# Moving the second gate's modulation vector from the first stage of an encoder layer into its feed-forward

## The chip, the cores and the metric

The kernel runs on one core of a Trainium2 chip. A core has TensorE (PE, matrix products; PEld is its weight load), VectorE (DVE), ScalarE (ACT), GpSimd (POOL) and SyncE (SP), whose queue issues nearly all DMA transfers here. The engines run side by side and wait for each other by semaphores. The metric is the device time of one execution in microseconds (us). Every difference below is against the median of the runs of the kernel before.

## The reference

One encoder layer on 2048 tokens of width 1024, all in float32. A conditioning vector c gives six vectors of 1024 numbers, of which the last, gate2, is the subject:

```
mod = silu(c) @ w_mod + b_mod                  # (1, 6*1024)
shift1, scale1, gate1, shift2, scale2, gate2 = split(mod, 6)
hmix = rms_norm(x, g_norm1) * (1 + scale1) + shift1
proj = hmix @ w_in                             # attention q, k, v; mLSTM q, k, v, o, gates
...                                            # windowed attention, two-way mLSTM, norms
x    = x + gate1 * (concat(att, h_m) @ w_out)
hff  = rms_norm(x, g_norm2) * (1 + scale2) + shift2
gte, up = split(hff @ w_ffn_in, 2)             # 1024 -> 2 x 2816
x    = x + gate2 * ((silu(gte) * up) @ w_ffn_out)
out  = rms_norm(x, g_final)
```

gate2 is needed by the last product alone. w_mod is 1024 x 6144; the part for one vector is 1024 x 1024 numbers, 4 MB.

## The kernel before

**Stages.** The token dimension is cut into 16 tiles of 128 (tt), or four blocks of 512 (n). The stages follow each other on TensorE: the norm with the "natural" products of the first stage (attention values, gates and mLSTM values, lines 277 to 489, until about 182 us of the profile); the other columns of w_in with the convolution, the mLSTM and the attention (to about 930 us); the output projection; the feed-forward's first product in two halves of 22 units each (`pair`, to about 1840 us); its second product.

Products keep float32 accuracy by splitting each operand into a rounded part hi and a remainder lo, and adding three products (`mm3`, lines 56 to 58): hi by hi, hi by lo, lo by hi. ScalarE makes hi, VectorE or POOL makes lo. Every operand made on the chip therefore costs a ScalarE and a VectorE (or POOL) instruction.

**The modulation vectors.** shift1 and scale1 are needed first and are made at the start (`mod_sum`). The other four are made by `mod_row(m)`, lines 359 to 395, where m is the number of the vector: 2 is gate1, 3 shift2, 4 scale2, 5 gate2. For each half z of 512 columns it loads four pieces of w_mod of 128 x 2 x 512 numbers, and VectorE adds up silu(c)[k] times row k in one tile of 128 x 512 (lines 373 and 375). This tile is split, and TensorE multiplies it by a matrix of ones (lines 381 and 382, tile modrow), which adds the 128 partitions. For a gate, VectorE adds the bias row (line 384) and the row goes to the DRAM tile gate_d (line 385). For the others, the row is turned into columns.

`mod_row` is a generator that yields after the split of each half. The loop over tt advances it once per token tile, behind the 48 products of that tile (line 485): gate1 in the tiles 4 to 6, then shift2, scale2 and gate2, from tile 8 on without tile 9. A half's two products with ones stand on TensorE behind the products of the tile that follows its split. gate2's two halves are split in the tiles 13 and 14, and their products stand behind the tiles 14 and 15, the last.

**What sets the order.** TensorE's order is that of the program in the whole kernel (`manual_schedule`). In the first stage, from line 439 on, the instructions of VectorE, ScalarE, POOL and SP are ordered by a planner that works at build time; so are those of the attention (lines 1010 to 1231). In the convolution and mLSTM (lines 971 to 1009), and from line 1232 on, which takes in the whole feed-forward, they follow the program. A call of a generator between two instructions thus says where on every engine's queue its instructions stand.

**Behind the first stage.** The first weight columns of the convolution are loaded by line 247 (tile wraw), rounded on ScalarE (line 251) and their remainder is made on POOL in four quarters (line 254). Line 839 transposes the gates of all tokens, and lines 498 are the convolution's products. POOL's preparation of w_out (lines 920 to 960) reads gate1 back from gate_d.

**A unit of the feed-forward.** `pair(hh, j, ws_, hop, ...)`, lines 1593 to 1660, computes 512 + 512 tokens of half hh for a pair of blocks of 128 columns by seven products of smaller operands (a Strassen-Winograd scheme), each of 4 x 3 = 12 matmuls. It uses three banks: ps1 takes products 0, 2, 4 and 6, ps2 product 1, ps5 products 3 and 5. Between the products the banks are read: line 1613 copies ps1 after product 0 (s), 1616 adds ps2 (g), 1619 copies ps1 after product 2 (u), 1624 copies ps5 after product 3 (c), 1627 ps1 after product 4, 1631 adds ps5 after product 5, 1640 multiplies ps1 after product 6. A bank that is added to again has to be read first. Two tanh, 1620 and 1632, with 1621 and 1633 behind them, form the activation. POOL does 1628, 1639 and 1645. Every second unit completes a pair of column blocks, and then POOL's 1654 to 1658 make further sums. The results go to the DRAM tile a_d; their stores are issued by `stores()` behind the next unit's product 0 (line 1590).

Beside the products, `beside(u)` (lines 1677 to 1697) is called behind each product u = 0 to 6. It advances `weights`, which makes the seven operands of the next unit (names A11, A12, S2, S1, S3, S4, A22; ScalarE line 1455, VectorE line 1456, POOL lines 1460 to 1467): one at u = 2 and 3, two at u = 4 and 5, one at u = 6. At u = 6 it also loads the raw weights of the unit after next. In the first half it also advances `norm2`, which uses the four buffers "xt" of 128 x 1024 in the pool ff; in the second half these lie unused until the second product's results.

gate_d's second row is read once, by line 1800, in the last unit (at 1841 us of the profile).

Of the kernel before, what the change touches and what calls it, by code (L numbers as in the profile page):

```python
# [11 lines left out]
F32 = mybir.dt.float32  # L12
F32R = mybir.dt.float32r
# [4 lines left out]
MUL, ADD, SUB, MAX, MIN = ALU.mult, ALU.add, ALU.subtract, ALU.max, ALU.min  # L18
# [3 lines left out]
P = 128  # L22
T = 2048
D = 1024
KT = D // P
# [11 lines left out]
def hybrid_layer_kernel(  # L37
# [14 lines left out]
    def bank(tag, name):  # L52
        return pp.tile([P, 512], F32, tag=tag, name=name, bufs={"g": 2, "a": 2, "b": 1, "c": 2, "d": 1}[tag])
# [86 lines left out]
    def split(src, hi, lo):  # L140
        act.activation(hi, src, AF.Copy)
        dve.tensor_tensor(lo, src, hi.bitcast(F32), SUB)
# [135 lines left out]
    with tc.tile_pool(name="sw", bufs=2, side="right", reuse_waits="tile") as sw:  # L278
# [20 lines left out]
        ps = bank("a", "colps")  # L299
# [59 lines left out]
        def mod_row(m):  # L359

            for z in range(2):
                acc = sw.tile([P, 512], F32, tag="macc", name="macc", bufs=1)
                if m in (2, 5):
                    br = (s1 if m == 2 else wp).tile([1, 512], F32, tag="mrow" if m == 2 else "oth", name="brow", bufs=1)
                    sp.dma_start(br, b_mod[:, m * D + z * 512:m * D + (z + 1) * 512])
                for k in range(0, KT, 2):
                    w = (hp if "b" in wrow[0] else sw if "m" in wrow[0] else wp).tile([P, 2, 512], F32, tag=wrow[0], name="wmod", bufs=1)
                    wrow.rotate(-1)
                    sp.dma_start(w, w_mod[k * P:(k + 2) * P, m * D + z * 512:m * D + (z + 1) * 512]
                                 .rearrange("(k p) c -> p k c", p=P))  # L370
                    for i in range(2):
                        if k + i == 0:
                            dve.tensor_scalar(acc, w[:, 0, :], sc_col[:, 0:1], None, MUL)
                        else:
                            dve.scalar_tensor_tensor(acc, w[:, i, :], sc_col[:, k + i:k + i + 1], acc, MUL, ADD)
                hi = sw.tile([P, 512], F32R, tag="macch", name="macch", bufs=1)
                lo = sw.tile([P, 512], F32R, tag="maccl", name="maccl", bufs=1)
                split(acc, hi, lo)
                yield True
                ps = bank("c", "modrow")  # L380
                pe.matmul(ps, ones_r, hi, start=True, stop=False)
                pe.matmul(ps, ones_r, lo, start=False, stop=True)
                if m in (2, 5):
                    dve.tensor_tensor(br, ps[:1, :], br, ADD)
                    sp.dma_start(gate_d[m // 5:m // 5 + 1, z * 512:(z + 1) * 512], br)
                    continue
                row = sw.tile([P, 512], F32, tag="macch", name="mrow", bufs=1)
                act.activation(row, ps, AF.Copy)
                for k in range(4):
                    rk = row[:, k * P:(k + 1) * P]  # L390
                    dve.tensor_tensor_reduce(out=rk, in0=rk, in1=ident, op0=MUL, op1=ADD, scale=1.0, scalar=0.0,
                                             accum_out=mod[:, m, 4 * z + k:4 * z + k + 1])
            if m not in (2, 5):
                o = O_BM + m * KT
                dve.tensor_tensor(mod[:, m, :], mod[:, m, :], cols[:, o:o + KT], ADD)

# [47 lines left out]
        for n in range(NB):  # L444
            if n + 1 < NB:
                nrm = norm1(n + 1, xts[n + 1])
                next(nrm)
            if n == 0:
                xts.append(load_x(3))
            if n == 1:  # L450
                vecs = mod_row(2)
                columns_of(1, N_A, N_B)
                dve.tensor_scalar(cvw, cols[:, O_CW:O_CW + 24].rearrange("p (j k) -> p j k", j=3), 0.5, None, MUL)
                dve.tensor_scalar(cvb, cols[:, O_CB:O_CB + KT], 0.5, None, MUL)
                dve.tensor_scalar(gml, cols[:, O_GM:O_GM + HM], 0.5, None, MUL)
            if n + 1 == NB:
                w_first = proj_cols(C_KM)
            for i in range(4):
                tt = 4 * n + i
                if tt < 3:  # L460
                    pa, pv = ops[i]
                else:
                    pa, pv = bank("g", "pa"), bank("a", "pv")
                ev = EVERY[n][i]
                for j, _ in enumerate(nat_mm(n, i, pa, pv, range(4 if tt < 3 else 0, KT))):
                    if ev and j % ev == ev - 1:
                        next(nrm, None)
                if tt == 8:
                    deque(nrm, 0)
                    wrow = deque(["w1h", "w1l", "wm0", "wm1"])  # L470
                    xs.close()
                    wp = ctx.enter_context(tc.tile_pool(name="w", bufs=1, side="left", reuse_waits="tile"))
                    wslots.extend([(wp, 0), (wp, 1)])
                    vecs = chain.from_iterable(mod_row(m) for m in range(3, 6))
                vs = sw.tile([P, KV, 2, HD], F32R, tag="vs", name="vs", bufs=1)
                va = sw.tile([P, HM, 129], F32, tag="va", name="va")
                pav = pa[:, :128].rearrange("p (k d) -> p k d", k=KV)
                act.activation(vs[:, :, 0, :], pav, AF.Copy)
                dve.tensor_tensor(vs[:, :, 1, :], pav, vs[:, :, 0, :].bitcast(F32), SUB)
                dve.tensor_tensor(gn[:, :, :, :, tt], pa[:, 128:144].rearrange("p (d y h) -> p y d h", d=2, y=2), bgv, ADD)  # L480
                act.activation(va[:, 0, :128], pa[:, 144:272], AF.Copy)
                act.activation(va[:, 1:, :128], pv[:, :384].rearrange("p (h d) -> p h d", d=128), AF.Copy)
                pool.memset(va[:, :, 128:129], 1.0)
                if tt != 9:
                    next(vecs, None)
                sp.dma_start(vst_d[tt * P:(tt + 1) * P], vs.bitcast(F32))
                sp.dma_start(vaug_d[tt * P:(tt + 1) * P], va)
# [1089 lines left out]
    with tc.tile_pool(name="ff", bufs=1, side="right", reuse_waits="tile") as ff:  # L1577
# [83 lines left out]

        pools["ff"] = ff
        pools["xp"] = xp
        norms = deque([norm2(1, 0, "bd", 4), norm2(1, 1, "bd", 1)])
        JO = [m * KH + j for j in range(KH) for m in range(2)]
        units = [(0, j) for j in JO] + [(1, j) for j in reversed(JO)]
        wseq = deque(JO[2:] + JO[-2::-1])
        raw, more_w = (*raws[0], load_a22(KH)), None
        for n, (hh, j) in enumerate(units[:-1]):
# [7 lines left out]
            def beside(u):  # L1677
# [17 lines left out]
                    raw = load_raw(wseq.popleft())  # L1695
                if n > 1 and u in (1, 3, 5) and norms and next(norms[0], None) is None:
                    norms.popleft()

            pair(hh, j, ws_, hop, start, beside)
            if turn:  # L1700
# [264 lines left out]
```

## Time and profile before

| | |
|---|---|
| median of 3 runs | 2272.53 us (2272.24 to 2273.72) |
| the profiled execution | 2272.8 us, its span 2271.0 us |
| TensorE busy | 2222.9 us (98% of the span) |
| VectorE, ScalarE, POOL busy | 1606.1, 1060.4, 1065.4 us |
| granted TensorE clock, mean | 0.995 |
| gate2's w_mod, loaded once | 8 transfers of 512 KB on SP |

The span is the time between the first and the last instruction that the profile shows; the time of the execution has a little around it. A busy share close to one says that the time can only change through that engine's own instructions and its remaining waits. The views used below give, for a line or a tile, how often and how long its instructions ran, and, in order of time, each engine's instructions with the idle time before them and what ended it.

### The profile page before, as it was taken

Reading aid. Unit: us, or ns where it says so; the run is one execution under the profiler, and the core shown is the slowest. Engines: PE = TensorE matmul, PEld = TensorE weight load, DVE = VectorE, ACT = ScalarE, POOL = GpSimd, SP = SyncE. Lnnn points to the kernel's source line nnn. Section 1 sums busy time; section 2 is a strip of 40 time slices with the busy share of each in tenths; the row PEclk is TensorE's granted clock in tenths of the full one; section 3 lists DMA queues with packets and bytes.
Section 4 is the critical chain, followed back from the end, with each engine's and each line's share of the span. In section 5 each row is a group of like instructions: output and inputs, shape, how many; then the busy total and the mean of one; then the engine's idle time right before and its main releaser. Section 6 shows DMA issues by size and latency. Waiting matters only on the chain.

```text
span 2271.0 us, 32441 instructions
## 1 busy us (share of the span) xinstructions
PE 2222.9 (98%) x10822; PEld 1857.2 (82%) x10822; DVE 1606.1 (71%) x2931; ACT 1060.4 (47%) x2206; POOL 1065.4 (47%) x927
## 2 busy tenths in 40 slices
PE   6999999999999999999999999999999999999998
PEld 4997888888888878788888888788888888888886
DVE  6787577656688887786767786766666666785694
ACT  5433655554677746354445444433333333233452
POOL 1006635334344334436666665666566654692020
PEclk9999999999999999999999999999999999999999
DMA  8476755585766575764343454433333374442462
GB/s 331 158 248 213 239 170 165 185 242 173 210 185 181 172 250 197 267 233 149 110 148 112 157 181 165 155 98 111 98 112 98 112 253 145 167 153 94 147 214 93
DMA packets 352811, 391.28 MB, mean 172 GB/s; under 512 B 21260, under 2 KB 251004, under 8 KB 352644
## 3 DMA queue, kind: packets, MB, share of 16 engines
q1 hardware_dynamic: 352420, 389.18, 52.4%
q8 instruction: 85, 1.39, 0.2%
q14 instruction: 82, 0.67, 0.1%
q10 hardware_dynamic: 224, 0.04, 0.0%
HBM read 269.95 MB, written 119.19 MB: 171 GB/s over the span
## 4 chain that ended last, share of the span: by engine, by line
PE 55%; DVE 2%; issue 1%; DMA 0%; ACT 0%; ACTq 0%; DVEq 0%
PE fp L56 12%; PE fp L57 12%; PE fp L58 12%; PE fo L58 6%; PE fo L56 6%; PE fo L57 6%; PE ops L56 1%; PE ops L57 1%; PE ops L58 1%; DMA T<-hop_d 0%; DVE ra L1862 0%; PE trn L183 0%; DVE T L1417 0%; DVE ra L1877 0%; DVE B L1417 0%
## 5 line engine op out<-in xcount | busy, mean ns | idle before, releaser
L498 PE MATMUL gps<-hT,whi 128*128 128x512 f32 x1088 | 395.7, 418 | 0.3 <-DVE cacc L513 0.3
L58 PE MATMUL fo<-w,al 128*128 128x512 f32 x616 | 239.8, 389 | 0.4 <-DVE al L1719 0.4
L57 PE MATMUL fo<-w,ah 128*128 128x512 f32 x616 | 239.7, 389 | 0.0
L56 PE MATMUL fo<-w,ah 128*128 128x512 f32 x616 | 239.7, 389 | 0.0
L498 PE MATMUL gps<-hT,wlo 128*128 128x512 f32 x544 | 226.1, 416 | 0.0
L498 PEld LDWEIGHTS gps<-hT,whi 128*128 128x128 f32 x1088 | 199.5, 190 | 24.2 <-DVE cacc L513 0.7
L56 PE MATMUL fp<-T,S 128*128 128x512 f32 x528 | 206.8, 392 | 0.6 <-ACT s L1613 0.6
L57 PE MATMUL fp<-T,S 128*128 128x512 f32 x528 | 205.7, 389 | 0.0
L58 PE MATMUL fp<-T,S 128*128 128x512 f32 x528 | 205.4, 389 | 0.0
L1719 DVE TENSOR_TENSOR al<-al,ah 128x1024 fp32r<-128x1024 f32 x77 | 116.5, 1518 | 108.4 <-ACT ah L1718 108.2
L1718 ACT ACTIVATE ah<-al 128x1024 fp32r<-128x1024 f32 x77 | 81.6, 1060 | 180.4 <-DMA al<-a_d 178.9
L1456 DVE TENSOR_TENSOR S<-sf,S 128x512 fp32r<-128x512 f32 x86 | 129.9, 1548 | 37.3 <-ACT S L1455 37.1
L1456 DVE TENSOR_TENSOR A<-graw,A 128x512 fp32r<-128x512 f32 x86 | 128.1, 1511 | 14.1 <-ACT A L1455 14.1
L58 PE MATMUL fp<-B,A 128*128 128x512 f32 x352 | 136.9, 389 | 0.0
L56 PE MATMUL fp<-B,A 128*128 128x512 f32 x352 | 136.9, 389 | 0.0
L57 PE MATMUL fp<-B,A 128*128 128x512 f32 x352 | 136.9, 389 | 0.0
L58 PEld LDWEIGHTS fo<-w,al 128*128 128x128 f32 x616 | 115.6, 188 | 24.9 <-DVE al L1719 0.8
L56 PEld LDWEIGHTS fo<-w,ah 128*128 128x128 f32 x616 | 115.7, 188 | 24.1
L57 PEld LDWEIGHTS fo<-w,ah 128*128 128x128 f32 x616 | 115.6, 188 | 23.9
L1621 DVE SCALAR_TENSOR_TENSOR g<-t,g 128x512 f32<-128x512 f32 x44 | 44.3, 1008 | 128.2 <-ACT t L1620 128.2
L798 POOL TENSOR_SCALAR ap<-ap,adn 128x384 f32<-128x384 f32 (+1 forms) x128 | 72.4, 587 | 126.7 <-PE atp L805 58.6
L1460 POOL TENSOR_TENSOR sf<-A,A22r 128x512 f32<-128x512 f32 x43 | 60.8, 1415 | 146.9 <-DMA A22r<-in_w_ffn_in_dram 122.3
(418 smaller groups left out, 6160.3 us busy)
## 6 DMA issues: line engine op xcount, KB each, us to landing
al<-a_d SPq DMA_DIRECT2D x77, 512.0 KB, 3.7
wmod<-in_w_mod_dram SPq DMA_DIRECT2D x48, 512.0 KB, 7.6
graw<-in_w_ffn_in_dram SPq DMA_DIRECT2D x43, 512.0 KB, 3.7
a_d<-ka SPq DMA_DIRECT2D x66, 256.0 KB, 4.6
bc<-bc_d SPq DMA_DIRECT2D x64, 256.0 KB, 3.7
hop_d<-n SPq DMA_DIRECT2D x56, 256.0 KB, 4.4
a_d<-u SPq DMA_DIRECT2D x55, 256.0 KB, 4.6
mqk<-qk_d SPq DMA_DIRECT2D x44, 256.0 KB, 3.9
```

The source lines that it names most:

```text
L56: pe.matmul(o, lh, rh, start=first, stop=False, skip_group_check=skip)
L57: pe.matmul(o, lh, rl, start=False, stop=False, skip_group_check=skip)
L58: pe.matmul(o, ll, rh, start=False, stop=last, skip_group_check=skip)
L498: pe.matmul(ps, w[i == 2][:, k, :], hT[n](i == 1, k), start=(k == 0 and i == 0), stop=(k == KT - 1 and i == 2))
L798: pool.tensor_scalar(self.p[g][:, :self.NK], self.p[g][:, :self.NK], dn[:, g:g + 1], 0.0, MUL, ADD)
L1456: dve.tensor_tensor(t[:, 1, :], f, t[:, 0, :].bitcast(F32), SUB)
L1460: pool.tensor_tensor(f1, a21, a22, ADD)
L1621: dve.scalar_tensor_tensor(g0, t0, 1.0, g0, ADD, MUL)
L1718: act.activation(ah, al.bitcast(F32), AF.Copy)
L1719: dve.tensor_tensor(al, al.bitcast(F32), ah.bitcast(F32), SUB)
```

## The change

`mod_row` is no longer called for m = 5, and no longer knows it. A new generator, `gate2`, computes the same vector in the feed-forward. It takes tiles of 128 x 1024 from the buffers "xt", loads w_mod in eight pieces of 128 x 1024 (all columns of 128 rows), adds them up in eight VectorE instructions of 1024 columns, splits the sum once, multiplies by ones in two halves (banks b and d) and stores the row in one transfer. `beside` advances it in the second half (n over NJ = 22, so from n = 23 on), behind the products u = 1 and u = 4 of each unit: a call at u = 1 issues a load, the call at u = 4 the multiplication. The split falls to u = 1 of n = 31, the four matmuls and two row additions to u = 4 of n = 31, the store to u = 1 of n = 32. In the first stage, nothing of gate2 is left, and the loop's calls in the tiles 14 and 15 find the generator exhausted.

```diff
@@ mod_row @@
-                if m in (2, 5):
-                    br = (s1 if m == 2 else wp).tile([1, 512], F32, tag="mrow" if m == 2 else "oth", name="brow", bufs=1)
+                if m == 2:
+                    br = s1.tile([1, 512], F32, tag="mrow", name="brow", bufs=1)
...
-                if m in (2, 5):
+                if m == 2:
                     dve.tensor_tensor(br, ps[:1, :], br, ADD)
-                    sp.dma_start(gate_d[m // 5:m // 5 + 1, z * 512:(z + 1) * 512], br)
+                    sp.dma_start(gate_d[0:1, z * 512:(z + 1) * 512], br)
                     continue
...
-                    vecs = chain.from_iterable(mod_row(m) for m in range(3, 6))
+                    vecs = chain.from_iterable(mod_row(m) for m in (3, 4))
@@ feed-forward @@
+        def gate2():
+
+            row = lambda n, dt=F32: ff.tile([P, D], dt, tag="xt", name=n, bufs=4)
+            wr, acc, br = [row("wmod") for _ in range(2)], row("macc"), row("brow")
+            sp.dma_start(br[:1, :], b_mod[:, 5 * D:6 * D])
+            for k in range(KT):
+                w = wr[k % 2]
+                sp.dma_start(w, w_mod[k * P:(k + 1) * P, 5 * D:6 * D])
+                yield True
+                if k == 0:
+                    dve.tensor_scalar(acc, w, sc_col[:, 0:1], None, MUL)
+                else:
+                    dve.scalar_tensor_tensor(acc, w, sc_col[:, k:k + 1], acc, MUL, ADD)
+                yield True
+            hi, lo = row("macch", F32R), row("maccl", F32R)
+            split(acc, hi, lo)
+            yield True
+            for z in range(2):
+                ps, zs = bank("bd"[z], "modrow"), slice(z * 512, (z + 1) * 512)
+                pe.matmul(ps, ones_r, hi[:, zs], start=True, stop=False)
+                pe.matmul(ps, ones_r, lo[:, zs], start=False, stop=True)
+                dve.tensor_tensor(br[:1, zs], ps[:1, :], br[:1, zs], ADD)
+            yield True
+            sp.dma_start(gate_d[1:2, :], br[:1, :])
+
         norms = deque([norm2(1, 0, "bd", 4), norm2(1, 1, "bd", 1)])
+        gate = gate2()
...
                 if n > 1 and u in (1, 3, 5) and norms and next(norms[0], None) is None:
                     norms.popleft()
+                if n > NJ and u in (1, 4):
+                    next(gate, None)
```

More of the change, by code (lines that the diff above doesn't have):

```diff
@@ L392, in mod_row @@
                                              accum_out=mod[:, m, 4 * z + k:4 * z + k + 1])
-            if m not in (2, 5):
+            if m != 2:
                 o = O_BM + m * KT
```

## Prediction

> **What bounds the kernel now.** I read first the busy time of each engine in long stretches of the span (columns: length; busy us and instructions of PE, PEld, DVE, ACT and POOL; granted clock; DMA share; GB/s). The rows are stage two up to the end of the attention, the feed-forward's second half, and the whole span.
>
> ```profile
> 182.00:930.00 748.00, 735.37 (x3970) 617.79 (x3970) 541.55 (x1560) 450.10 (x1200) 335.57 (x443) 1.00 0.66 203
> 1446.00:1840.00 394.00, 393.39 (x1736) 325.43 (x1735) 259.79 (x250) 152.07 (x273) 246.02 (x162) 1.00 0.34 113
> 0.00:2271.00 2271.00, 2222.89 (x10822) 1857.15 (x10822) 1606.05 (x2931) 1060.37 (x2206) 1065.38 (x927) 1.00 0.53 172
> ```
>
> TensorE is busy for 2222.9 of 2271.0 us. In the second half, where the vector goes, it idles 0.6 us in 394, and its matmuls follow each other at 394 / 1736 = 0.227 us. So the time changes only by TensorE's waits and by its own instructions. The question is how many idle microseconds the vector causes where it is now, and how many it will cause there.
>
> Then the instructions on the tile wmod (times in ns, minimum, median, maximum):
>
> ```profile
> L375 DVE SCALAR_TENSOR_TENSOR macc<-wmod,sc_col,macc x56: 729/751/1107, 82.3 to 177.3; 128x512 f32<-128x512 f32 x56
> L369 SPq DMA_DIRECT2D wmod<-in_w_mod_dram x32: 367/381/911, 60.5 to 169.1; - x32
> ...
> DMA to landing us min/median/max: 4.3/7.6/10.3
> ```
>
> Four vectors share L375, 14 each. One vector is thus 14 of these, 2 first products, 8 loads of 512 KB. Of this VectorE work (14 x 0.75, about 11 us) none is TensorE's. What TensorE sees is the end of each half: it multiplies the summed tile by ones, in program order between two blocks of products, and waits for ScalarE and VectorE to split the sum. TensorE in order of time, the last two such places (start, duration, what, idle before):
>
> ```profile
> 169.06 0.33 PE L58 MATMUL pv<-wnh,hT 128*128 128x384 f32 x1
> 169.86 0.50 PE L381 MATMUL modrow<-macch,ones_r 128*128 128x512 f32 x1 [0.47 <-ACT macch L141]
> 170.58 0.50 PE L382 MATMUL modrow<-maccl,ones_r 128*128 128x512 f32 x1 [0.23 <-DVE maccl L142]
> 170.92 0.29 PE L56 MATMUL pa<-wnh,hT 128*128 128x272 f32 x1
> ...
> 177.96 0.33 PE L58 MATMUL pv<-wnh,hT 128*128 128x384 f32 x1
> 179.27 0.50 PE L381 MATMUL modrow<-macch,ones_r 128*128 128x512 f32 x1 [0.98 <-ACT macch L141]
> 180.11 0.50 PE L382 MATMUL modrow<-maccl,ones_r 128*128 128x512 f32 x1 [0.34 <-DVE maccl L142]
> 180.45 0.38 PE L839 MATMUL gps<-ident,gn 128*128 128x128 f32 x2
> ```
>
> Both are the second gate's halves. The products end at 169.39 and 178.29 and go on at 170.92 and 180.45: 1.53 + 2.16 = 3.69 us.
>
> **The change part by part. Stage one.** Removed: 8 weight loads, 2 bias loads and 2 stores on SP, 16 wide VectorE instructions, 2 splits, 2 row additions, 4 matmuls. The value is the 3.69 us above, all of it on TensorE. What is late next? The first weight tile of the convolution: loaded on SP, rounded on ScalarE, its remainder made on POOL in four quarters (each a row of SP, ScalarE and POOL in order of time).
>
> ```profile
> 172.55 0.43 SPq L247 DMA_DIRECT2D wraw<-in_w_in_dram  x1
> ```
> ```profile
> 177.64 1.06 ACT L251 ACTIVATE whi<-wraw 128x1024 fp32r<-128x1024 f32 x1 [0.74 <-DMA wraw<-in_w_in_dram]
> ```
> ```profile
> 178.78 3.35 POOL L254 TENSOR_TENSOR wlo<-wraw,whi 128x256 fp32r<-128x256 f32 x4 [11.68 <-ACT whi L251]
> ```
>
> Its first quarter is ready at 178.78 + 3.35 / 4 = 179.62. TensorE would reach L839 at 180.45 - 3.69 = 176.76 and use that quarter some 0.7 us later (two transposes and two products first), at 177.44. If nothing on SP moves, it waits 2.2 us. But this load stands on SP behind the gate's own loads and its store, which are gone. If it is issued 2.2 us sooner nothing is lost. Bounds 0 and 2.2; I take 0.3, near the first, because an in-order queue loses eight loads and two stores ahead of or around it. Stage two behind it follows TensorE's own first transposes (L839), so it moves along.
>
> **The matmuls, put back.** Four in the second half, behind the fifth product of a unit: 4 x 0.227 = 0.91 us, on the path. Their operands are made half a unit earlier, so no wait of their own.
>
> **The loads, put back.** Eight of 512 KB, one per unit of 84 matmuls (84 x 0.227 = 19.1 us), issued on SP in the second of a unit's seven products, behind that unit's stores; the multiplication stands in the fifth, three products (8.2 us) later, and a load took 7.6 us in stage one at its much busier DMA, where the second half has a DMA share of 0.34. What is queued behind a load on SP is the next raw weights, four products later. Bias load and store: two more issues. In the unit after a completed pair the stores go out about when L1620 runs (1586.2 in the rows below), so the load would land at 1593.8 and VectorE come to it at 1594.6: covered, but only just; at the longest landing shown, 10.3 us, VectorE would wait 1.9 us in such a unit. I cost the loads at nothing; the cover is these 8 us.
>
> **VectorE, put back.** Per unit one multiply-add of 128x1024: 2 x 0.72 (midway between L375 above and the 0.69 of L1633 below), 1.45 us; the first of the eight is a plain multiplication; one unit has a split and two row additions instead. VectorE is busy 259.8 of 394 us, so on the average there is room. But it stands at a bad place: behind the two S splits, ahead of L1631. One unit (its VectorE, POOL and ScalarE rows):
>
> ```profile
> 1591.20 3.48 DVE L1456 TENSOR_TENSOR S<-sf,S 128x512 fp32r<-128x512 f32 x2
> 1594.61 0.68 DVE L1631 TENSOR_TENSOR u<-fp,u 128x512 f32<-128x512 f32 x1
> 1596.04 0.69 DVE L1633 SCALAR_TENSOR_TENSOR u<-t,u 128x512 f32<-128x512 f32 x1 [0.76 <-ACT t L1632]
> ```
> ```profile
> 1592.38 1.74 POOL L1467 TENSOR_TENSOR graw<-graw,sf 128x512 f32<-128x512 f32 x1
> 1596.87 1.62 POOL L1639 TENSOR_TENSOR ka<-c,u 128x512 f32<-128x512 f32 x1 [2.74 <-issue]
> ```
> ```profile
> 1586.22 0.63 ACT L1620 ACTIVATE t<-g 128x512 f32<-128x512 f32 x1 [1.02 <-DMA a_d<-u]
> ...
> 1587.32 0.60 ACT L1624 ACTIVATE c<-fp 128x512 f32<-128x512 f32 x1
> ...
> 1590.04 0.60 ACT L1627 ACTIVATE u<-fp 128x512 f32<-128x512 f32 x1 [1.60 <-PE fp L58]
> ...
> 1595.38 0.63 ACT L1632 ACTIVATE t<-u 128x512 f32<-128x512 f32 x1 [3.70 <-DVE u L1631]
> ...
> 1598.20 0.60 ACT L1613 ACTIVATE s<-fp 128x512 f32<-128x512 f32 x1 [0.62 <-PE fp L58]
> ```
>
> L1631 had no idle before it, so it moves by the whole 1.45 us. ScalarE's L1632 waits for it, and behind L1632 on ScalarE stand three roundings and then L1613, which empties the next unit's first bank. TensorE adds to that bank again two products later. L1613 had 0.62 us of idle; the bank was full at about 1598.0, and with 12 matmuls (2.72 us) of the second product TensorE wants it empty at 1600.72.
>
> Units go in twos. The unit that completes a pair of column blocks stores its difference (a_d<-u); L1620 of the unit after it waits for that store to land. So a delay of 1.45 in the first reaches L1620 of the second through L1640, POOL's L1645 and SP, and the second adds its own 1.45: its L1613 comes at 1598.20 - 0.62 + 2.9 = 1600.48 and ends at 1601.08, so TensorE waits 0.36 us. L1624 moves by 1.45 only: 1587.92 + 1.45 = 1589.37, before L1627's product ends at about 1589.8, no wait. In the unit after, VectorE catches up in the 3 to 4 us it waits for L1620. Right behind the turn of the halves there is less slack:
>
> ```profile
> 1461.58 1.76 POOL L1467 TENSOR_TENSOR graw<-graw,sf 128x512 f32<-128x512 f32 x1
> ```
> ```profile
> 1484.39 0.58 ACT L1613 ACTIVATE s<-fp 128x512 f32<-128x512 f32 x1
> ```
>
> That L1613 has no idle at all (six units before 1598.20 would be 1484.0), and in the unit before it POOL still runs while the first multiplication would stand (to 1463.3). This L1613 ends at 1484.97, and is wanted by 1483.8 + 2.72 = 1486.5: 1.5 us of slack against 1 to 2 us inherited and 1.45 of its own, so I take 1.4 us of wait. The four pairs: 1.4 + 3 x 0.36 = 2.5 us. Bounds: 0, if the neighbours give way, and twice it.
>
> Here a rule is weighed against a row. L1633 reads two float32 tiles in SBUF, multiplies and adds, in 0.69 us for 512 columns, as long as the plain addition L1631. The Trainium skill's Vector Engine (DVE) Microarchitecture Reference, section Points that are easy to get wrong, says that this form with two SBUF sources that are not bf16 runs at half throughput. By the rule at its 0.96 GHz an estimate for 1024 columns is 2.1 us, and the four pairs would cost some 5 us more; the row speaks against it, and the chance is in rival two.
>
> The sum: 2272.8 (the profiled execution, span 2271.0) - 3.69 + 0.3 + 0.91 + 2.5 = 2272.8; that execution was 0.27 above the median of 2272.53, so 2272.5 against the median, which is no change.
>
> **The rivals.** One, all of VectorE's and ScalarE's added work is hidden: no wait in the second half. For it speaks the 0.6 us of idle in 394; against it the chain L1631 to L1613. It gives 2272.53 - 3.69 + 0.91 = 2269.8.
>
> Two, slower: the multiply-add is long. Its narrower relation in the same code:
>
> ```profile
> L1621 DVE SCALAR_TENSOR_TENSOR g<-t,g x44: 681/766/1822, 1003.5 to 1833.3; 128x512 f32<-128x512 f32 x44
> ```
>
> The same instruction takes 0.68 to 1.82 us; L1456, at 1.74 each beside POOL's L1467 above and 0.68 elsewhere, suggests POOL as the reason. At duration s the wait of a pair grows by 2 (s - 1.45), of four pairs by 8 (s - 1.45). To lose 4.5 us it takes 4.5 = 8 (s - 1.45), s = 2.01 us; at s = 2.3 the time is 2272.5 + 6.8 = 2279.3, and at twice 1.82 it would be 2290. Against it: POOL stands idle for 2.74 us before L1639, and the new instruction falls in that gap, since L1639 waits for L1633 behind it. The Trainium skill's SBUF — State Buffer, section Who interferes with whom, has VectorE and GpSimd hold one pair of ports exclusively in turn; by that rule the gap is what decides, and the trace agrees (0.68 beside idle POOL, 1.74 beside busy).
>
> Three, faster by more than forecast: the freed VectorE, SP and DMA time in stage one (DMA busy there) starts stage two's side work earlier, and of the 748 - 735.4 = 12.6 us that TensorE idles until 930 a quarter goes, 3 us: 2269.8 - 3 = 2266.8. For it: the order of VectorE, ScalarE, POOL and SP in stage one is made by a planner and will change; against it: these waits are single ones of about 1 us in the scans and in the attention, far from this place.
>
> **How the numbers follow.** Chances: the forecast 0.52, one 0.22, two 0.15, three 0.09, anything else 0.02. The forecast's own range is 2269.8 to 2276.9 (no waits, or twice those counted, 2.5, and the late weight tile, 1.9, on top). A measurement tells 0.2% (4.5 us) from no change: 2268.0 to 2277.1. The forecast and rival one lie inside, two and three mostly outside. Range for 8 in 10: 2267.5 to 2278.0. Faster 0.10, same 0.75, slower 0.15.
>
> **What would show it.** Stage one: after the block of token tile 13 no modrow matmul stands between products, and L839 starts near 177. Second half: four modrow matmuls near 1609, L375's successor at about 1.45 us for 1024 columns, TensorE waits on L1613 (ACT s) of 0.3 to 1.5 us in every second unit between 1470 and 1600. Wrong: multiply-adds of over 2 us, VectorE idle for a wmod load, waits on L1624, or a first convolution that waits for wlo.

## The result, and the profile after

| | before | changed |
|---|---|---|
| median | 2271.96 us (12 runs, 2269.29 to 2274.20) | 2278.70 us (12 runs, 2274.80 to 2283.11) |
| profiled execution, its span | 2272.8 us, 2271.0 us | 2279.26 us, 2277.5 us |

The ratio is 1.0027, with a 95% interval of 1.0019 to 1.0034 (4.3 to 7.7 us). The medians differ by 6.7 us: the changed kernel is slower where no change was forecast, and its median is 0.7 us above the end of the range.

Where the time went is seen from two marks that both kernels have: the last transposition of x1t (line 183) in the first half of the feed-forward, and the first product of the last stage (tile fo). Before (groups of TensorE's instructions, with the first and last start):

```profile
L183 PE MATMUL trn<-ident,x1t x64: 270/272/273, 1123.9 to 1341.1; 128*128 128x128 f32 x64
L56 PE MATMUL fo<-w,ah x616: 387/389/398, 1842.8 to 2261.9; 128*128 128x512 f32 x154
```

And the changed kernel:

```profile
L183 PE MATMUL trn<-ident,x1t x64: 270/272/273, 1122.3 to 1339.6; 128*128 128x128 f32 x64
L56 PE MATMUL fo<-w,ah x616: 389/389/394, 1850.0 to 2268.5; 128*128 128x512 f32 x154
```

Between the marks lie 1842.8 - 1341.1 = 501.7 us before and 1850.0 - 1339.6 = 510.4 after. I call this stretch the second half; it lost 8.7 us. Everything ahead of it gained 1341.1 - 1339.6 = 1.5 us in these two executions, where the prediction had 3.4; the last stage is 0.7 us shorter (427.5 against 428.2 to the end of the span). 8.7 - 1.5 - 0.7 = 6.5 us is the difference of the spans.

The changed kernel's second half and span, as the rows of before were shown (length; busy us of PE, PEld, DVE, ACT, POOL; granted clock):

```profile
1446.00:1848.00 402.00, 396.38 (x1735) 324.86 (x1736) 269.11 (x260) 150.34 (x270) 244.63 (x162) 1.00 0.37 121
0.00:2277.50 2277.50, 2224.70 (x10822) 1857.20 (x10822) 1602.36 (x2922) 1058.83 (x2205) 1066.69 (x927) 1.00 0.53 172
```

TensorE now idles 402 - 396.4 = 5.6 us in the second half, where it was 0.6. What it waits for there (us in total, times, longest), in the changed kernel:

```profile
PE fp L56 <- ACT c L1624: 4.3, 5, 1.7
PE fp L56 <- ACT s L1613: 0.8, 2, 0.5
```

Most of the loss is behind L1624, the copy of bank ps5, which the prediction had ruled out. Idle time is not all: a stop also costs about 0.25 us until the matmuls follow at 0.227 us again. With every gap between two starts counted over 0.227, the changed kernel loses 7.8 us more than the one before, and the four matmuls, which stand in a row as forecast, add 4 x 0.23:

```profile
1614.70 0.40 PE L1684 MATMUL modrow<-macch,ones_r 128*128 128x512 f32 x1
...
1615.40 0.39 PE L1685 MATMUL modrow<-maccl,ones_r 128*128 128x512 f32 x1
```

7.8 + 0.9 = 8.7 us, the whole loss of the second half.

**One of the waits, followed back.** The longest ends at 1515.38, in unit n = 26. The rows of all engines of the changed kernel in order of time, from the unit before it:

```profile
1496.68 2.80 DVE L1456 TENSOR_TENSOR S<-sf,S 128x512 fp32r<-128x512 f32 x2 [1.86 <-ACT S L1455]
1498.90 1.74 POOL L1467 TENSOR_TENSOR graw<-graw,sf 128x512 f32<-128x512 f32 x1
1499.41 2.31 DVE L1677 SCALAR_TENSOR_TENSOR macc<-wmod,sc_col,macc 128x1024 f32<-128x1024 f32 x1
1501.64 0.68 DVE L1631 TENSOR_TENSOR u<-fp,u 128x512 f32<-128x512 f32 x1
...
1506.00 0.68 DVE L1640 TENSOR_TENSOR u<-fp,g 128x512 f32<-128x512 f32 x1
...
1506.82 1.61 POOL L1645 TENSOR_TENSOR u<-u,c 128x512 f32<-128x512 f32 x1 [1.29 <-DVE u L1640]
1508.41 1.41 SPq L1590 DMA_DIRECT2D a_d<-u  x2
...
1513.69 0.63 ACT L1620 ACTIVATE t<-g 128x512 f32<-128x512 f32 x1 [4.86 <-DMA a_d<-u]
...
1514.74 0.58 ACT L1624 ACTIVATE c<-fp 128x512 f32<-128x512 f32 x1
...
1515.38 0.50 PE L56 MATMUL fp<-B,S 128*128 128x512 f32 x1 [1.75 <-ACT c L1624]
```

The same place before:

```profile
1495.99 2.39 DVE L1456 TENSOR_TENSOR S<-sf,S 128x512 fp32r<-128x512 f32 x2 [1.07 <-ACT S L1455]
1497.79 1.74 POOL L1467 TENSOR_TENSOR graw<-graw,sf 128x512 f32<-128x512 f32 x1
1498.30 0.68 DVE L1631 TENSOR_TENSOR u<-fp,u 128x512 f32<-128x512 f32 x1
...
1502.65 0.68 DVE L1640 TENSOR_TENSOR u<-fp,g 128x512 f32<-128x512 f32 x1
...
1510.32 0.63 ACT L1620 ACTIVATE t<-g 128x512 f32<-128x512 f32 x1 [1.28 <-DMA a_d<-u]
...
1511.38 0.58 ACT L1624 ACTIVATE c<-fp 128x512 f32<-128x512 f32 x1
...
1513.68 0.39 PE L56 MATMUL fp<-B,S 128*128 128x512 f32 x1
```

The step takes from 1499.41 to 1501.64, 2.23 us, and not the 1.45 assumed. The S splits ahead of it start 0.69 later and last 0.41 longer. Together L1631 is 3.34 us later than before, L1640 3.35, L1620 3.37, L1624 3.36: the delay passes undiminished through POOL, the store, its landing and ScalarE. Before, L1624 started 2.30 us ahead of the product that needs it; a released product starts 0.64 us behind L1624's start (1515.38 - 1514.74), so 1.66 us were to spare (the slack), and 1.45 in the changed kernel, whose TensorE was here 0.21 us ahead. 3.36 - 1.45 = 1.91 us, which is what TensorE lost.

Why 2.3 us? POOL's L1467 runs from 1498.90 to 1500.64 beside it. In the changed kernel, as a group (ns, minimum, median, maximum):

```profile
L1677 DVE SCALAR_TENSOR_TENSOR macc<-wmod,sc_col,macc x7: 1273/1273/2314, 1481.4 to 1601.7; 128x1024 f32<-128x1024 f32 x7
```

The three that took 2.31 stand in the units 25, 27 and 29, the four of 1.27 in 24, 26, 28 and 30. The odd ones are those that complete a pair of column blocks, and only their work on POOL and their stores hold up the next unit. What L1620 waits for last is not always the landing: in unit 28 it was POOL's L1658 (3.67 us), which stands on POOL behind the same late L1645.

### The profile page after: what moved, and what is told of

It reads as the page before. It is cut to its first block, busy times and chain, and to the rows that moved or that the text cites. A ratio compares the mean times of both kernels' runs of the same rounds, so it can differ in the third digit from the quotient of the medians.

```text
span 2277.5 us, 32413 instructions
## 1 busy us (share of the span) xinstructions
PE 2224.7 (98%) x10822; PEld 1857.2 (82%) x10822; DVE 1602.4 (70%) x2922; ACT 1058.8 (46%) x2205; POOL 1066.7 (47%) x927
## 4 chain that ended last, share of the span: by engine, by line
PE 51%; DVE 3%; DMA 1%; issue 1%; ACT 1%; POOL 1%; SPq 0%; POOLq 0%; ACTq 0%; DVEq 0%
PE fp L56 10%; PE fp L57 10%; PE fp L58 10%; PE fo L57 6%; PE fo L58 6%; PE fo L56 6%; DVE S L1456 1%; DMA a_d<-u 1%; PE ops L56 1%; PE ops L58 1%; PE ops L57 1%; DVE A L1456 1%; DVE macc L1677 0%; DMA T<-hop_d 0%; PE trn L183 0%
## 5 line engine op out<-in xcount | busy, mean ns | idle before, releaser
L1456 DVE TENSOR_TENSOR S<-sf,S 128x512 fp32r<-128x512 f32 x86 | 129.1, 1539 | 43.6 <-ACT S L1455 43.3
L1456 DVE TENSOR_TENSOR A<-graw,A 128x512 fp32r<-128x512 f32 x86 | 126.0, 1484 | 18.1 <-ACT A L1455 18.0
```

Source lines behind the costliest of these rows:

```text
L1456: dve.tensor_tensor(t[:, 1, :], f, t[:, 0, :].bitcast(F32), SUB)
```

## The experiments

Second half: the stretch between the two marks in each kernel's profile. Times are medians. Each run had its own runs of the kernel before beside it, so the ratio is to be compared, not the time.

The stretch also holds one or two stops of 0.5 to 1.6 us at the turn of the halves, ahead of gate2's first step, which come and go from execution to execution (two before, one in e1, e5, e6 and e11). So a difference of about 1 us in it means little. The last column leaves them out: it counts the gaps of TensorE over 0.227 us behind unit 22 alone, above those of the kernel before, without the four matmuls.

| kernel | time | ratio to before, 95% | second half | waits behind unit 22, us |
|---|---|---|---|---|
| before | 2270.7 to 2272.0 | | 501.7 | 0 |
| changed | 2278.70 | 1.0027 (1.0019 to 1.0034) | 510.4 | 8.2 |
| e1, step shifted by half a unit | 2269.38 | 0.9989 (0.9980 to 0.9998) | 501.1 | 0.0 |
| e2, feed-forward part alone | 2282.47 | 1.0043 (1.0031 to 1.0056) | 511.1 | 8.9 |
| e3, first-stage part alone | 2272.64 | 1.0003 (0.9994 to 1.0011) | 500.8 | 0.0 |
| e4, L251 held back | 2277.59 | 1.0024 (1.0015 to 1.0033) | 511.0 | 8.2 |
| e5, even units only | 2271.78 | 1.0003 (0.9994 to 1.0012) | 502.9 | 1.5 |
| e6, odd units only | 2276.17 | 1.0024 (1.0013 to 1.0034) | 507.4 | 6.2 |
| e7, VectorE's work without its loads | 2278.36 | 1.0037 (1.0024 to 1.0050) | 508.9 | 6.5 |
| e8, loads without the multiply-adds | 2273.10 | 1.0009 (0.9998 to 1.0019) | 504.5 | 2.8 |
| e9, own buffer for t | 2275.62 | 1.0022 (1.0012 to 1.0032) | 506.6 | 4.3 |
| e10, e9 and e1 | 2268.73 | 0.9988 (0.9979 to 0.9996) | 502.0 | 0.0 |
| e11, odd units, half the columns | 2273.50 | 1.0005 (0.9995 to 1.0014) | 502.0 | 0.8 |

### The two parts, and the place

e1 leaves out the first call, so that every later one falls half a unit later: the load behind product 4, the multiplication behind product 1 of the next unit, where VectorE waits for ScalarE's tanh.

```diff
-                if n > NJ and u in (1, 4):
+                if n > NJ and u in (1, 4) and (n, u) != (NJ + 1, 1):
                     next(gate, None)
```

> The second half's calls of gate2 are shifted by half a unit: a load is issued at u = 4 and its multiplication stands at u = 1 of the next unit, where VectorE waits 3 to 6 us for the tanh of L1620 anyway. Theory one (the place: the multiplication ahead of L1631 delays the store of the difference, the raw weights and with them L1624 and L1613, 7.7 us of lost TensorE time): the lost time falls to under 2 us, and the time to 2271 to 2274 us. Theory two (the amount of work or the added loads: VectorE or the DMA queues are too full in this half): 2277 us or more, with waits on L1624 as before.

e2 is the kernel before with the changed kernel's feed-forward: `gate2` and its calls added, `mod_row(5)` kept.

```diff
+        def gate2():
...
+        gate = gate2()
...
+                if n > NJ and u in (1, 4):
+                    next(gate, None)
```

> The kernel before, with its first stage as it is, and gate2 of the change computed a second time in the feed-forward. Theory one: all of the loss is in the second half, the time is that of before plus 7.7 us of waits plus 0.9 us of matmuls, 2279 to 2282 us. Rival (the new order of stage one makes a part of the loss): no more than 2277 us.

e3 is the changed kernel with nothing left in `gate2` but the bias row and its store.

```diff
-            for k in range(KT):
...
-                dve.tensor_tensor(br[:1, zs], ps[:1, :], br[:1, zs], ADD)
             yield True
             sp.dma_start(gate_d[1:2, :], br[:1, :])
```

> The changed kernel without the products of gate2: its row is the bias alone, so the vector's loads, sums and matmuls are left out everywhere. It shows what stage one gives. By the changed profile, where the first feed-forward product starts 1.5 us earlier than before although the first 50 us were 1.4 to 2 us longer: 2268.5 to 2271 us. If the stage-one gain were whole (3.69 us): 2268 us. Rival (stage one lost by its new order): 2272 us or more.

Measured: e1 gives back the whole loss of the second half, with the same loads, VectorE instructions and matmuls. In unit 26 its step runs behind L1616 at 1499.87 for 1.38 us, inside an idle stretch, and L1620 and L1624 keep their slack. The view of waits lists none of TensorE's behind unit 22. e1's time lies below the range that was expected (2269.38 against 2271 to 2274). e2 has the loss of the second half alone, 9.4 us by the marks and 10.9 by the medians, 0.5 us over its range. e3's median stands 1.0 us above the one of before, with an interval of -1.4 to +2.5 us: it falls to the rival, and taking the vector out of the first stage brought nothing there that could be measured. So the place of VectorE's step made the loss. What the first stage gives is less clear, because e1 and e10, with the same first stage as e3, came out 2.2 and 3.2 us below the kernel before.

### Which units, and how long the step

e5 and e6 advance `gate2` in every second unit only. They differ in one digit.

```diff
-                if n > NJ and u in (1, 4):
+                if n > NJ and u in (1, 4) and n % 2 == 0:
```

> The changed kernel with gate2 advanced in every second unit of the feed-forward's second half only, in the units 24, 26, ... 38 (split and matmuls in 40, store in 42): the same eight loads and VectorE steps, at the same places behind the products u = 1 and u = 4, but only in units that do not complete a pair of column blocks. Theory A (the delay reaches TensorE through the completing unit: its L1640 is late, so are POOL's L1645 and the store of u, on whose landing the next unit's L1620 waits, and L1624 stands behind it): no wait on L1624 beside the two of before, at most some on L1613, feed-forward's second half 501 to 504 us, time 2269 to 2273 us. Theory B (each step costs its own delay wherever it stands): second half 509 to 511, time 2277 to 2280. Theory C (only the accumulation over units in sequence costs, through the late raw weights; a free unit between lets VectorE catch up): about 502 and 2271 here and in the run with the other units alike.

> The same, but in the units 23, 25, ... 37 (split in 39, store in 41), the ones that complete a pair. Theory A: eight completing units are delayed instead of four, each costs a wait on L1624 of 0.8 to 1.2 us in the unit behind it, 6 to 10 us in all: second half 508 to 512 us, time 2276 to 2281 us. Theory B: 509 to 511, 2277 to 2280, as in the run with the other units. Theory C: about 502, 2271.

In e5 (even units) VectorE's steps and TensorE's waits behind unit 22 are:

```profile
L1677 DVE SCALAR_TENSOR_TENSOR macc<-wmod,sc_col,macc x7: 1271/1272/1274, 1519.8 to 1746.9; 128x1024 f32<-128x1024 f32 x7
```
```profile
PE fp L56 <- ACT c L1624: 0.2, 1, 0.2
```

In e6 (odd units):

```profile
L1677 DVE SCALAR_TENSOR_TENSOR macc<-wmod,sc_col,macc x7: 2305/2314/2318, 1497.3 to 1730.4; 128x1024 f32<-128x1024 f32 x7
```
```profile
PE fp L56 <- ACT c L1624: 3.1, 4, 1.5
```

The same eight steps cost 1.2 us of second half in one kind of unit and 5.7 in the other; behind unit 22 alone the waits are 1.5 and 6.2 us. A cost per step (B) and a mere pile-up from unit to unit (C) both fall. A holds, though e6 lost a little less than it said (507.4 us is under its range, 2276.17 at its lower end), and TensorE waited behind four of the eight units only. The rows show a second difference: every step in an odd unit takes 2.31 us, every one in an even unit 1.27. So length and path could still each be the cause. Two runs part them.

e11 is e6 with the multiply-adds cut to 512 columns; they stay in the odd units.

```diff
-                    dve.scalar_tensor_tensor(acc, w, sc_col[:, k:k + 1], acc, MUL, ADD)
+                    dve.scalar_tensor_tensor(acc[:, :512], w[:, :512], sc_col[:, k:k + 1], acc[:, :512], MUL, ADD)
...
-                if n > NJ and u in (1, 4):
+                if n > NJ and u in (1, 4) and n % 2 == 1:
```

> The run in the units 23, 25, ... 37 with the seven multiply-adds cut to 512 of 1024 columns, so half of the vector is not gate2's. There each took 2.31 us, because POOL's L1467 was still running for about 1 us of it, and 1.27 us in the other units. If a step starts in earnest only when POOL's instruction ends, half the columns take 1.6 to 1.8 us, and the waits on L1624 (slack about 1.5 us) fall from 4.7 us to under 2: second half 503 to 505 us, time 2271 to 2274 us. If the number of steps counts, not their length: 507, 2276 as with all columns.

e11's steps:

```profile
L1677 DVE SCALAR_TENSOR_TENSOR macc<-wmod,sc_col,macc x7: 1775/1779/1781, 1502.0 to 1730.2; 128x512 f32<-128x512 f32 x7
```

Half the columns take 1.78 us: 0.69 (L1633, the same form and width with POOL idle) + 1.09. All the columns take 2.31 = 1.27 + 1.04. e8 (below, under the loads) has steps of 8 columns at the places of the changed kernel; the short ones stand in the even units, the long ones in the odd:

```profile
L1677 DVE SCALAR_TENSOR_TENSOR macc<-wmod,sc_col,macc x7: 214/215/1256, 1479.9 to 1595.2; 128x8 f32<-128x8 f32 x7
```

1.26 = 0.21 + 1.05. The addition does not grow with the width. In the rows of unit 25 above, L1467 had 1.23 us left when the step began, so the three widths fit an instruction that waits for POOL's L1467 to end and then runs at its usual speed. The Trainium skill's SBUF — State Buffer, section Who interferes with whom, says that VectorE with two SBUF inputs and GpSimd hold a pair of ports exclusively, and that the loser is blocked for the other's whole instruction; these rows agree.

With 0.5 us less per step the waits on L1624 fall below what the view of waits lists, and the second half from 507.4 to 502.0, as a slack of about 1.5 us would have it. By the medians the loss falls from 5.4 to 1.5 us. (The waits on L1624 in e6 were 3.1 us by the view above, not the 4.7 of the expectation.) A part of this is not the width's. Behind unit 23, whose first product is equally long in both, e6 waits 0.56 us and e11 does not; and in unit 26 the time from L1645's start to L1620's was 7.0 us in e6 and 6.3 in e11.

e9 leaves the changed kernel's steps where they are and takes L1620 out of the path: the tile t of the first tanh gets a buffer of its own, so that L1620 does not wait for a store to land.

```diff
-            s1_, g0, t0, u2, c5, u3 = (ot(n) for n in ("s1", "g0", "t0", "u2", "c5", "u3"))
+            s1_, g0 = ot("s1"), ot("g0")
+            t0 = tx[0][:, :512] if tx else ot("t0")
+            u2, c5, u3 = ot("u2"), ot("c5"), ot("u3")
...
-            wr, acc, br = [row("wmod") for _ in range(2)], row("macc"), row("brow")
-            sp.dma_start(br[:1, :], b_mod[:, 5 * D:6 * D])
+            wr, acc = [row("wmod") for _ in range(2)], row("macc")
+            tx.append(row("t0"))
...
             split(acc, hi, lo)
+            br = row("brow")
+            sp.dma_start(br[:1, :], b_mod[:, 5 * D:6 * D])
```

> The changed kernel, its VectorE work at the same places, but the tile t, which the first tanh of a unit (L1620) writes, gets a buffer of its own in the second half (half of a buffer xt; the bias row is loaded later, into the buffer of the finished sum, to make room). L1620 then no longer waits for the landing of the store of u. Theory A (the chain runs L1640, POOL's L1645, store of u, its landing, L1620, L1624): no or few waits on L1624, the waits on L1613 stay (1 to 3 us), feed-forward's second half 502 to 505 us, time 2271 to 2274 us. Rival: another buffer of the same ring takes the wait over (L1619 or L1624 itself waits for a landing), second half 508 to 511, time 2277 to 2280.

TensorE's waits behind unit 22 in e9, its steps, and ScalarE in unit 24 (L1615, L1622 and L1626 are L1613, L1620 and L1624, two lines further down):

```profile
PE fp L56 <- ACT s L1615: 2.3, 4, 0.8
PE fp L56 <- ACT c L1626: 0.2, 1, 0.2
```
```profile
L1679 DVE SCALAR_TENSOR_TENSOR macc<-wmod,sc_col,macc x7: 2308/2314/2320, 1478.1 to 1595.7; 128x1024 f32<-128x1024 f32 x7
```
```profile
1467.41 0.62 ACT L1622 ACTIVATE t<-g 128x512 f32<-128x512 f32 x1
...
1471.02 0.60 ACT L1626 ACTIVATE c<-fp 128x512 f32<-128x512 f32 x1 [1.91 <-DMA a_d<-u]
```

TensorE's waits on L1624 went from 4.3 to 0.2 us. The path was shortened and not taken away: as the rival had it, L1626 now waits for the landing itself (1.76 to 1.91 us in the units 24, 28 and 30), or for POOL's three sums (2.05 us in unit 26). But L1622 and a rounding, 1.05 us in the rows of unit 26 above, no longer stand between the landing and it, and it comes early enough. So the path through L1645, the store and L1620 is shown. Less was gained than I expected (506.6 and 2275.62, not 502 to 505 and 2271 to 2274). In e9 every step starts 0.51 us behind L1467, in the even units too, so all seven take 2.31 us, and TensorE waits on the other chain, L1631, L1632, L1613, which the prediction described. The likely reason is that the stop at L1620, which parted POOL and VectorE in the even units, is gone.

e10 is e9 with e1's line.

> The same buffer for t together with the shift of VectorE's step by half a unit (load behind u = 4, multiplication behind u = 1 of the next unit). If the shift alone has removed all that VectorE's step costs, the buffer brings nothing more: second half 500 to 502 us, time 2267 to 2271 us, as with the shift alone. If the store of u held TensorE in the units of the first tiles still, up to 1 us less.

With the step in VectorE's idle stretch the buffer brings nothing more: 2268.73 against e1's 2269.38, and 502.0 against 501.1. Both are about 0.1% faster than the kernel before.

### The loads

e7 issues the first two loads only, and the later steps read these tiles again; e8 issues all and shrinks the multiply-adds.

```diff
-                sp.dma_start(w, w_mod[k * P:(k + 1) * P, 5 * D:6 * D])
+                if k < 2:
+                    sp.dma_start(w, w_mod[k * P:(k + 1) * P, 5 * D:6 * D])
```

> The changed kernel with the first two of the eight loads alone; the later multiply-adds read these two tiles again, so the vector is not gate2's. VectorE's work, TensorE's four matmuls and all places stay. If VectorE's place is the cause: second half 508 to 511 us, time 2276 to 2280 us, waits on L1624 as in the changed kernel. If the loads are (they delay the raw weights on the same queue or by their share of the DMA engines): second half 501 to 504, time 2269 to 2273.

```diff
-                    dve.scalar_tensor_tensor(acc, w, sc_col[:, k:k + 1], acc, MUL, ADD)
+                    dve.scalar_tensor_tensor(acc[:, 0:8], w[:, 0:8], sc_col[:, k:k + 1], acc[:, 0:8], MUL, ADD)
```

> The changed kernel with all eight loads and the first product, but with the seven multiply-adds cut to 8 of 1024 columns, so the vector is not gate2's. If VectorE's place is the cause: one wait on L1624 behind the first product (about 1.1 us at 1475), then few: second half 502 to 505 us, time 2269 to 2274 us. If the loads are: second half 508 to 511, time 2276 to 2280.

e7 loses as the changed kernel does (7.6 us by the medians, against 6.7). Its profile has somewhat less: 6.5 us of waits behind unit 22, against 8.2 to 8.9 in the three with all loads. e8 loses 2.8 us of second half, 0.9 of it matmuls, and its waits are two:

```profile
PE fp L56 <- ACT c L1624: 1.7, 2, 1.2
```

The longer one is behind the first product, which is left at full width in unit 23 and took 1.78 us beside L1467 (0.74 in e5, in unit 24). The other, 0.5 us, is behind unit 25, whose step of 8 columns still met L1467 and took 1.26 us. The loads are thus not the main cause. That they cost something by slower landings stays possible, up to the 2 us by which e7's profile is better; e5 has a wait of 0.2 us in unit 24, ahead of its first step. It was not tried apart.

### The first stage

In the changed kernel the planner issues the convolution's first weight tile at 155.77 us instead of 172.55 and puts its rounding (L251) ahead of the last split (L141) on ScalarE. The changed kernel, all engines in order of time, and TensorE's granted clock behind it:

```profile
163.44 1.06 ACT L251 ACTIVATE whi<-wraw 128x1024 fp32r<-128x1024 f32 x1 [2.39 <-DMA wraw<-in_w_in_dram]
...
164.56 0.62 ACT L141 ACTIVATE macch<-macc 128x512 fp32r<-128x512 f32 x1
...
165.23 0.49 PE L381 MATMUL modrow<-macch,ones_r 128*128 128x512 f32 x1 [2.10 <-ACT macch L141]
...
165.96 0.78 PE L382 MATMUL modrow<-maccl,ones_r 128*128 128x512 f32 x1 [0.23 <-DVE maccl L142]
```
```profile
166.50:169.20 2.70, 2.70 (x13) 2.67 (x12) 1.59 (x10) 0.60 (x1) 1.48 (x3) 0.50 0.24 91
169.20:172.00 2.80, 2.80 (x21) 2.80 (x20) 0.38 (x2) 0.47 (x2) 0.00 (x0) 0.96 0.01 3
```

TensorE waits 2.10 us for a modrow product of scale2, which waited for nothing before, and then runs 2.7 us at a clock of 0.50: 13 matmuls where the next 2.8 us at 0.96 hold 21. L839 starts at 182.3 us, not near 177. That is the worst of ten profiled executions with this first stage: L839 starts at 177.4 to 182.3 us in them, 179.0 on the mean, against 180.4 and 180.8 in the two with the first stage of before.

e4 holds L251 back until behind the last row of scale2 (L388).

```diff
-            if n + 1 == NB:
-                w_first = proj_cols(C_KM)
             for i in range(4):
+                if (n, i) == (NB - 1, 2):
+                    with tc.issue_after(last_row[4, 1]): w_first = proj_cols(C_KM)
```

> The changed kernel, with ScalarE's rounding of the first convolution weights (L251) held behind the last copy of scale2's row (L388) in ScalarE's order. Theory: in the changed kernel L251 waited for its load ahead of L141, which cost TensorE 2.1 us of waiting and then 1.2 us at a granted clock of 0.50; both go, L839 starts 3 us earlier, and the time is 2275 to 2276.5 us. Rival (those waits are absorbed by later ones): 2278 us or more.

The wait went, and L839 started at 175.4 us, 5 us ahead of before. But nothing of it was left when the attention began (L805 at 591.6 us, 590.8 before). From L839 to L805 e4 takes 416.2 us, where the other profiles take 407.5 to 412.9. Behind L839 TensorE waits for the gates of the mLSTM, a chain on VectorE that now ends last. Its waits between 183 and 200 us, and the stretches with the clock:

```profile
PE cps L892 <- DVE rw L885: 1.4, 1, 1.4
PE rps L871 <- DVE gates L866: 1.2, 1, 1.2
PE cps L892 <- DVE rw L886: 0.9, 1, 0.9
PE cps L893 <- ACT rw L888: 0.7, 1, 0.7
```
```profile
180.00:190.00 10.00, 8.61 (x40) 6.39 (x39) 9.71 (x17) 2.50 (x4) 7.68 (x8) 1.00 0.55 179
190.00:200.00 10.00, 6.94 (x26) 5.22 (x25) 8.73 (x15) 2.31 (x7) 8.44 (x11) 0.82 0.28 91
200.00:210.00 10.00, 10.00 (x40) 8.10 (x39) 4.94 (x12) 5.01 (x14) 4.67 (x5) 0.84 0.69 218
```

VectorE is busy for 18.4 of these first 20 us. What TensorE saves in front of it, it waits for here, and then runs at a lower clock. That explains where the gain went in this execution, which took 2282.61 us, 5 us over e4's median. The median, 2277.59, lies between what the theory and the rival had said, and the ratio is hardly below that of the changed kernel. Why e3 kept nothing while e1, with the same first stage, came out 3.3 us lower is open: their profiles part by single waits of under 1 us between 190 and 590 us, and one profile each does not say whether these are the rule.

## Why the prediction was wrong

**What bounds the kernel: right.** The time changed by TensorE's waits and its own instructions, and the whole loss is found in them.

**Stage one, -3.69 and +0.3: about half, if that.** Over the profiles L839 moved by some 1.6 us (179.0 against 180.6), and e3 shows no gain in time. The question "What is late next?" was put to the weight tile alone. That tile was early, and TensorE never waited for it; being early, its rounding pushed itself ahead of L141. "Stage two behind it follows TensorE's own first transposes (L839), so it moves along" held on the mean of the ten profiles (410.5 us to L805, against 410.4 and 410.0 before), but not in e4's: the gates' chain on VectorE behind L839 was not looked at, and it sets a limit. What the first stage gave in the end stays open between e3 (nothing) and e1 and e10.

**Four matmuls, +0.91: right.** They stand 0.23 us apart with no wait of their own.

**Loads, nothing: right as far as can be told.** VectorE waits for no wmod tile, and e7 without six of them is as slow by its median; up to 2 us are not ruled out.

**VectorE, +2.5: the term that failed, 7.8 measured.** Three steps of its working fell. First, 1.45 us a step: the multiply-add is quicker (1.27), but it takes 2.31 where POOL runs. The Trainium skill's Vector Engine (DVE) Microarchitecture Reference, section Points that are easy to get wrong, would have had it at half throughput everywhere, by the prediction's estimate at 2.1 us. The even units do not agree: 1.27 us for 1024 columns, and 0.69 for 512, as long as a plain L1456 with two inputs (0.68). Second, the sentence against rival two, "POOL stands idle for 2.74 us before L1639, and the new instruction falls in that gap": that was read from one unit, n = 30, which does not complete a pair. In the completing units 23, 25 and 29 of the kernel before POOL's L1467 ends later than the S splits, and the gap is not free; in unit 27 it is. The row for it stood in the profile of before (unit 25, L1467 until 1499.53 beside L1631 at 1498.30, above). The prediction had even seen it for unit 23 ("POOL still runs while the first multiplication would stand"), and took it for a matter of the turn of the halves. Third, "L1624 moves by 1.45 only ... no wait": L1640, the store and L1620 were seen as a chain, but its delay was taken as 1.45, and is 3.36 in the unit shown, against a slack of 1.45 there and 1.9 in the unit that was read. The slack itself was about right.

"In the unit after, VectorE catches up" also failed: the S splits of the completing unit already started 0.69 us late in the rows above. The likely way is the raw weights, whose single buffer is loaded anew when VectorE's last split has read it; that was not tried apart.

**The rivals.** Rival two gave 2279.3, and 2278.70 came. Its condition, a step over 2.01 us because POOL is in the way, was met in the completing units alone. That its number fits is in part luck: it priced all the steps at 2.3 us, through L1613, and the loss came from every second one, for the most part through L1624. Rival one describes e1, by another place. Rival three's gain of 3 us in stage two did not come: the stretch from L839 to L805 is as long as before on the mean.

## What to carry to other kernels

Before work is put on an engine's queue, look at every kind of iteration that the loop has, not at one, and ask what the neighbour that can block it is doing in just that slot; here the same instruction took 1.27 or 2.31 us by the parity of the unit. Then follow the delay to the first buffer that comes back through memory, compare it with the slack there, and if it does not fit, look for the engine's own idle stretch: half a unit later the same work cost nothing. And ask what chain of another engine stands behind a gain: in e4's profile TensorE came 5 us earlier to the gates and waited for them instead.

## What the runs showed of the hardware beyond this

TensorE's clock fell here after pauses of under 3 us. A wait of 2.10 us and one of 0.23 with a single product between them were followed by 2.7 us at 0.50 (above). In e7 the same place waited 2.40 us, in e8 1.41; the stretches from 160 to 170 us, e7 first:

```profile
160.00:170.00 10.00, 7.39 (x40) 6.65 (x39) 2.65 (x13) 3.27 (x7) 3.39 (x5) 0.83 0.10 34
```
```profile
160.00:170.00 10.00, 8.37 (x52) 7.69 (x52) 3.85 (x16) 3.27 (x7) 3.65 (x6) 1.00 0.19 64
```

With 2.40 us the clock fell, with 1.41 it did not. The length of one pause does not decide alone: in e4 (above) none was over 1.43 us, but three of 1.43, 0.94 and 0.69 us fell between 193 and 197 us, and the clock was 0.82 and 0.84. The Trainium skill's TensorE: Matmul & The Clock Gate, section Part 1: The HAM clock gate, has the clock halved after an idle window of about 3.4 us; the halving agrees, but here less idle time was enough. In the second half no stop was over 1.75 us, and the clock stayed at 1.00 (first row of the changed kernel above).
